# Retention queries projected ahead of the gates, attention's first keys and queries in memory of their own, pools waited for tile by tile, modulation sums spread

## The chip, the cores and the metric

The kernel runs on one core of a Trainium2 chip. A core has TensorE (PE, matrix products; its weight loads are listed as PEld), VectorE (DVE), ScalarE (ACT), GpSimd (POOL) and SyncE (SP, which here only issues DMAs), each with its own instruction stream that it works off in order, and 16 DMA engines that all queues share. The metric is the device time of one execution in microseconds (us).

## The reference

One layer of a diffusion backbone over 1024 latent tokens of width 1024, with 256 context tokens in front:

```
h      = rms_norm(x) * (1 + sc1) + sh1            # sc, sh, g: six vectors of silu(c) @ w_mod + b_mod
rq rk rv rg dq dk dv = split(h @ w_in)            # seven blocks of 512 columns, latents and context
y_ret  = silu(rg) * (retention forward + retention backward, each group-normed)   # 4 heads, chunks of 128
y_diff = subln((softmax(q1 k1) - lam * softmax(q2 k2)) @ v)                       # 4 heads, 1280 keys
x      = x + g1 * ([y_ret, y_diff] @ w_out)
x      = x + g2 * conv_ffn(rms_norm(x) * (1 + sc2) + sh2)                         # 1024 -> 2 x 2816 -> 1024
out    = rms_norm(x)
```

Retention walks through the chunks with a 128x128 state per head and direction: the forward and backward outputs of a chunk need its query, key, value, the state before it and the gate. The change touches only the part up to the end of the attention; the arithmetic stays the same.

## The kernel before, in words

Every product in float32 precision is made of three passes of 128x512 matmuls over a high and a low half of each operand (`passes`, L129 to L131). One tile of 128x512 outputs takes 8 x 3 of them.

**The first phase** (to about 100 us) computes two of the six modulation vectors (`pr`, `pm`), turns the latents (`px`), makes `hT`, the modulated input, and block 2 of `w_in` (retention values, tiles `pn`).

**The projections.** A block of `w_in` is streamed as four slices: a DMA into `raw` (2 buffers, pool `wr`), a cast on ACT to `whi` (L184) and a subtraction on DVE to `wlo` (L185), 5 buffers of that pair in pool `wp`. `natural` makes tiles with tokens on partitions and hands each to a finisher (`store_to`: one ACT copy, one DMA); `transposed` makes tiles with channels on partitions, which for queries and keys go through `rotated` (four ACT copies of 32 partitions, or two of 64, L419, and three DVE operations, L422 to L424; for the attention a cast on ACT, L410, and a subtraction on DVE, L411, too). All results go to DRAM. The blocks run in the order 5 (attention keys), 6 (attention values), 1 (retention keys), 3 (gates), 0 (retention queries), 4 (attention queries).

**Work beside the projections.** `beside(generator, rate)` gives a generator that much of a step for every group of three passes. `states_before` (backward states) runs beside block 3, `outputs` (the 32 retention steps) beside blocks 0 and 4, at 1.2 parts per group; a step has three parts. A step loads its query and key (`qk`) and its value and gate (`kvgf`), scores on PE (`pc`), decays on DVE (`sc`), multiplies with value and state (`po`), updates the state on PE and DVE (`puf`, `Sf`), and is gated on DVE and POOL (`o`, `ss`, `y`), turned (`pyt`) and stored (`yrd`). POOL makes `qq`, `ks`, the power for `ss`, and `y`.

**Modulation.** `modulation2(i)` for the other four vectors loads eight 512 KB pieces (`wm2`, 2 buffers), sums them on DVE into `macc` (1 buffer) and reduces over partitions on PE (`pg`) at once.

**The attention** has 32 units (4 heads of 8 query tiles): scores for the two maps (`pA`, one PSUM tile of 3 banks each), minimum on DVE (`mt`), exponential on ACT (`p`), their difference on DVE, turned on PE (`pt`), times the values (`pv`), normed and turned (`pty`). Their order is a table of phases. `load` fetches queries (`qhl`), keys (`ks`) and values (`va`) of a head on POOL's queue. The last `TAIL` = 2 tiles of block 4 are projected after the first unit's scores have been asked for.

**What sets the order.** A scheduler in the build places each engine's instructions (outside of stretches that `in_order` fixes) by priority and its own estimate of when operands are ready. Memory is given by pools stacked on a left and a right side; a pool opened where others were closed waits, as a whole, for those others.

## Time and profile before

| | us |
|---|---|
| median of 3 runs | 1436.45 |
| lowest, highest | 1434.34, 1439.01 |
| the profiled execution, its own time | 1439.18 |
| its span | 1437.4 |
| PE busy | 1378.5 (96%) |
| DVE, ACT, POOL busy | 1007.2, 732.1, 369.4 |

Busy time is the time an engine's records cover; matmuls are pipelined with modelled ends, so a covered PE can still run slowly. `PEclk` in a view by stretches is the clock granted to TensorE, 1.00 at full speed. A row of waits gives who waited, for what, the total in us, how often and the longest. In a timeline, the bracket behind a row has the engine's idle time before it and what ended it. By place in the program: first phase 0 to 103 us, projections to 350, projections with retention to 482, start of the attention to 517, attention to about 690, then output projection and feed-forward to the end.

### The profile page before, as it was taken

How to read it: one execution, taken by the hardware profiler on the slowest of the kernel's cores; microseconds unless marked ns; L12 is line 12 of the kernel's file. 1: busy time of each engine (PE TensorE's matmuls, PEld its weight loads, DVE VectorE, ACT ScalarE, POOL GpSimd, SP SyncE). 2: the span in 40 equal slices, each digit the busy share in tenths (PEclk: the TensorE clock that was granted, in tenths of full speed). 3: DMA queues.
4: the chain of work that ended last, by engine and by line, in shares of the span. 5: the costliest groups of instructions: out<-in, count | busy, mean ns of one | idle time of the engine just before them, and what ended most of it. 6: DMA issues, size and time to landing. Idle time of an engine off the chain costs nothing.

```text
span 1437.4 us, 19423 instructions
## 1 busy us (share of the span) xinstructions
PE 1378.5 (96%) x6924; PEld 1144.8 (80%) x6924; DVE 1007.2 (70%) x1499; ACT 732.1 (51%) x1398; POOL 369.4 (26%) x467
## 2 busy tenths in 40 slices
PE   6999999999899989999999999999999999999997
PEld 3678788787778779999888777888888888888886
DVE  3578724333577589889346997787777777998756
ACT  3535512322456588998314654555555445455433
POOL 1230000021788323431121143222232220024003
PEclk9999999999999999999999999999999999999999
DMA  8448765465455667570522223332223324963324
GB/s 334 154 161 272 262 200 188 135 198 183 136 169 180 185 153 167 139 151 1 198 74 88 73 82 110 110 110 91 87 95 110 110 96 157 397 215 116 132 96 147
DMA packets 106377, 217.77 MB, mean 152 GB/s; under 512 B 8804, under 2 KB 47204, under 8 KB 104360
## 3 DMA queue, kind: packets, MB, share of 16 engines
q1 hardware_dynamic: 98152, 191.62, 39.0%
q0 software_dynamic: 8128, 24.91, 7.6%
q8 instruction: 55, 0.90, 0.3%
q14 instruction: 42, 0.34, 0.1%
HBM read 159.08 MB, written 57.41 MB: 151 GB/s over the span
## 4 chain that ended last, share of the span: by engine, by line
PE 77%; DVE 8%; DMA 5%; issue 3%; POOL 3%; ACT 3%; SPq 0%; POOLq 0%; DVEq 0%; ACTq 0%
PE chain L129 5%; PE chain L130 5%; PE chain L131 5%; PE c L130 5%; PE c L131 5%; PE c L129 5%; PE pv L765 5%; PE pA L733 5%; PE pn L131 3%; PE pn L129 3%; PE pn L130 3%; PE third L130 2%; PE third L129 2%; PE third L131 2%; PE pt L753 2%
## 5 line engine op out<-in xcount | busy, mean ns | idle before, releaser
L129 PE MATMUL chain<-T,whi 128*128 128x512 f32 x264 | 103.7, 394 | 6.8 <-ACT ua L1135 4.3
L129 PE MATMUL pl<-hT,whi 128*128 128x512 f32 x256 | 107.2, 419 | 1.2 <-ACT whi L184 1.2
L130 PE MATMUL chain<-T,whi 128*128 128x512 f32 x264 | 103.5, 392 | 0.0
L131 PE MATMUL chain<-T,wlo 128*128 128x512 f32 x264 | 103.1, 391 | 0.0
L131 PE MATMUL pl<-hT,wlo 128*128 128x512 f32 x256 | 100.7, 394 | 0.3 <-DVE wlo L185 0.3
L130 PE MATMUL pl<-hT,whi 128*128 128x512 f32 x256 | 100.7, 393 | 0.0
L736 DVE TENSOR_REDUCE mt<-pA 128x1 f32<-128x1280 f32 x64 | 95.3, 1490 | 3.6 <-PE pA L733 2.0
L733 PE MATMUL pA<-ks,qhl 128*128 128x512 f32 (+1 forms) x384 | 92.0, 376 | 4.8 <-ACT p L740 4.8
L1048 POOL TENSOR_TENSOR cmb<-wrb 128x512 f32<-128x512 f32 x20 | 27.4, 1372 | 250.8 <-DMA wrb<-w_up 158.2
L131 PE MATMUL c<-whi,ghl 128*128 128x512 f32 x232 | 90.4, 390 | 0.0
L129 PE MATMUL c<-whi,ghl 128*128 128x512 f32 x232 | 90.3, 389 | 0.0
L130 PE MATMUL c<-wlo,ghl 128*128 128x512 f32 x232 | 90.3, 389 | 0.0
L740 ACT ACTIVATE p<-pA,mt 128x1280 f32<-128x1280 f32 x64 | 85.5, 1336 | 4.5 <-DVE mt L736 4.5
L899 ACT CAST whi<-cmb 128x512 fp32r<-128x512 f32 x62 | 38.6, 622 | 88.1 <-PE chain L130 65.2
L733 PEld LDWEIGHTS pA<-ks,qhl 128*128 128x128 f32 x384 | 69.2, 193 | 17.6 <-ACT p L740 5.9
L129 PE MATMUL pn<-whi,hT 128*128 128x512 f32 x192 | 80.0, 416 | 2.4 <-ACT hT L575 2.4
L765 PE MATMUL pv<-va,aT 128*128 128x128 f32 x640 | 77.0, 275 | 0.1
L131 PE MATMUL pn<-whi,hT 128*128 128x512 f32 x192 | 75.3, 396 | 1.6 <-DVE hT L577 0.9
L899 ACT CAST whi<-wra 128x512 fp32r<-128x512 f32 x55 | 33.7, 622 | 83.5 <-PE third L130 42.3
L130 PE MATMUL pn<-wlo,hT 128*128 128x512 f32 x192 | 75.8, 395 | 0.0
L765 PEld LDWEIGHTS pv<-va,aT 128*128 128x128 f32 x640 | 74.0, 192 | 0.7 <-DVE yT L794 0.3
L900 DVE TENSOR_TENSOR wlo<-cmb,whi 128x512 fp32r<-128x512 f32 x62 | 57.8, 934 | 23.7 <-ACT whi L899 23.7
(320 smaller groups left out, 3915.0 us busy)
## 6 DMA issues: line engine op xcount, KB each, us to landing
wm<-w_mod SPq DMA_DIRECT2D x32, 512.0 KB, 4.3
raw<-w_in SPq DMA_DIRECT2D x28, 512.0 KB, 4.3
wra<-w_up SPq DMA_DIRECT2D x24, 512.0 KB, 3.3
wrb<-w_up SPq DMA_DIRECT2D x23, 512.0 KB, 3.6
W<-w_down SPq DMA_DIRECT2D x44, 256.0 KB, 6.3
ad<-s SPq DMA_DIRECT2D x20, 512.0 KB, 3.6
wra<-ad SPq DMA_DIRECT2D x20, 512.0 KB, 3.3
wrb<-ad SPq DMA_DIRECT2D x18, 512.0 KB, 3.3
```

What stands on the lines that cost most here:

```text
L129: mm(ps, lh, rh, start=first, stop=False, skip_group_check=more)
L130: mm(ps, lh, rl, start=False, stop=False, skip_group_check=more)
L131: mm(ps, ll, rh, start=False, stop=last, skip_group_check=more)
L733: mm(self.pa[m][:, c0:c1], self.q[:, i, m, qs], self.k[:, m, c0:c1], start=(i == 0), stop=(i == 1))
L736: nc.vector.tensor_reduce(out=self.mt[:, m : m + 1], in_=self.pa[m][:, :LK], axis=AX.X, op=ALU.min)
L740: nc.scalar.activation(self.p[m], self.pa[m][:, :LK], AF.Exp, scale=-1.0, bias=self.mt[:, m : m + 1], accum_out=self.s[:, m : m + 1])
L753: nc.tensor.transpose(self.pt[g][:, i, :], self.p[0][:, (4 * g + i) * P : (4 * g + i + 1) * P], ident)
L765: mm(self.pv, self.aT[:, c, :], self.v[:, c, :], start=(c == 0), stop=(c == NKT - 1))
L899: nc.scalar.copy(hi, src)
L900: nc.vector.tensor_tensor(out=lo, in0=src, in1=r32(hi), op=ALU.subtract)
L1048: nc.gpsimd.tensor_tensor(out=s1, in0=b1, in1=b2, op=ALU.add)
```

## The change

- Block order becomes 5, 6 (context only), 1, 0, 3, 6 again (latents only), 4. So the retention queries are made before the gates, and the attention values of the latents are made beside the retention steps (rate 1.05 in place of 1.2). Block 6 is loaded and split twice.
- While blocks 5, 6, 1 and 0 run, pool `m2p` lends one more `raw` buffer and one more `whi`/`wlo` pair (3 and 6 in place of 2 and 5).
- `modulation2` only sums; `modulated2` does the reduction as a generator beside later projections. `macc` has 2 buffers, `wm2` 3.
- `raw_latents` loads all four tiles before it normalizes the first.
- Many pools get `reuse_waits="tile"`: a tile waits only for what lay at its own place.
- The attention's queries, keys and values get pools of their own (`aq0`, `aq1`, `ak0`, `ak1`, `av`) at the places where the weight buffers and retention states lay; three of the four state tiles move to a pool `sb`. The PSUM pools `pst1` and `psb1` swap sides, and the last four tiles of block 4 use only the two `psa1` banks.

```diff
+        raw_pools = [lambda: wr] * 2
+        slice_pools = [lambda: wp] * 5
         def split_slice(src):
-            raw = wr.tile([P, 2, 512], F32, name="raw")
+            n = next(n_slices)
+            raw = raw_pools[n % len(raw_pools)]().tile([P, 2, 512], F32, name="raw")
             nc.sync.dma_start(out=raw, in_=src)
-            whi = wp.tile([P, 2, 512], F32R, name="whi")
-            wlo = wp.tile([P, 2, 512], F32R, name="wlo")
+            pool = slice_pools[n % len(slice_pools)]()
+            whi = pool.tile([P, 2, 512], F32R, name="whi")
+            wlo = pool.tile([P, 2, 512], F32R, name="wlo")
...
-            acc = m2p.tile([P, D], F32, name="macc")
+            maccs[i] = acc = m2p.tile([P, D], F32, name="macc", bufs=2)
...
+        def modulated2(i):
+            acc = maccs.pop(i)
             if i in (0, 3):
...
+                    yield
...
             def raw_latents():
+                xs = []
                 for t in range(4):
-                    xt = xp.tile([P, D], F32, name="xt", bufs=5)
-                    nc.sync.dma_start(out=xt, in_=x[t * P : (t + 1) * P, :])
-                    yield
+                    xs.append(xp.tile([P, D], F32, name="xt", bufs=5))
+                    nc.sync.dma_start(out=xs[t], in_=x[t * P : (t + 1) * P, :])
+                yield
+                for t, xt in enumerate(xs):
                     normalize(xt, 2 + t)
...
-        m2p = m2c.enter_context(tc.tile_pool(name="m2p", bufs=1))
+        m2p = m2c.enter_context(tc.tile_pool(name="m2p", bufs=1, reuse_waits="tile"))
+        raw_pools.append(lambda: m2p)
+        slice_pools.append(lambda: m2p)
         rtab = load_rope(1)
         wg = stream_block(5)
+        modulation2(0)
...
-        modulation2(1)
         transposed(wg, dk_d, rtab, 32, 1.0, LC, by_head[3:])
         wg = stream_block(6)
+        beside(modulated2(0), 0.1)
         natural(wg, ctx_lhs, range(NTC), store_to(dv_row))
-        modulation2(0)
-        natural(wg, lat_lhs, range(NT), store_to(dv_row, c0=NTC))
...
         wg = stream_block(1)
+        rtab = load_rope(0)
+        natural(wg, ctx_lhs, range(NTC), store_to(kvg_row(0), scale=RET_SCALE))
+        beside(iter(()), 0.0)
+        modulation2(1)
+        transposed(wg, [q[:, 1] for q in rqk_d], rtab, 64, RET_SCALE, 0, by_head[:5], True)
+        beside(modulated2(1), 0.4)
         modulation2(2)
-        natural(wg, ctx_lhs, range(NTC), store_to(kvg_row(0), scale=RET_SCALE))
+        transposed(wg, [q[:, 1] for q in rqk_d], rtab, 64, RET_SCALE, 0, by_head[5:], True)
+        wg = stream_block(0)
+        beside(modulated2(2), 0.25)
         modulation2(3)
+        transposed(wg, [q[:, 0] for q in rqk_d], rtab, 64, 1.0, 0, by_head[:6])
+        beside(modulated2(3), 0.2)
+        transposed(wg, [q[:, 0] for q in rqk_d], rtab, 64, 1.0, 0, by_head[6:])
...
-        transposed(wg, [q[:, 1] for q in rqk_d], rtab, 64, RET_SCALE, 0, by_head, True)
+        sb = rtx.enter_context(tc.tile_pool(name="sb", bufs=H - 1, side="right", reuse_waits="tile"))
         wg = stream_block(3)
         beside(states_before(), 36 / 62)
         natural(wg, lat_lhs, range(NT), store_to(kvg_row(2), func=AF.Silu, c0=NTC))
-        wg = stream_block(0)
-        beside(outputs(), 1.2, -12.0)
-        transposed(wg, [q[:, 0] for q in rqk_d], rtab, 64, 1.0, 0, by_head)
+        wg = stream_block(6)
+        beside(outputs(), 1.05, -12.0)
+        natural(wg, lat_lhs, range(NT), store_to(dv_row, c0=NTC))
         rtab = load_rope(1)
         wg = stream_block(4)
-        transposed(wg, dq_d, rtab, 32, -DIFF_SCALE, 0, by_head[:-TAIL])
+        transposed(wg, dq_d, rtab, 32, -DIFF_SCALE, 0, by_head[: -TAIL - 2])
+        mm_tiles[0] = itertools.cycle([ps_a])
+        transposed(wg, dq_d, rtab, 32, -DIFF_SCALE, 0, by_head[-TAIL - 2 : -TAIL])
...
-        al = aload.enter_context(tc.tile_pool(name="al", bufs=2, side="right"))
+        aq0, ak0, av, aq1, al, ak1 = (loads(*args) for args in (("aq0",), ("ak0",), ("av", 2), ("aq1",), ("al", 2), ("ak1",)))
...
-                cur["k"] = al.tile([P, 2, LK], F32R, name="ks")
+                cur["k"] = (ak0, ak1)[h % 2].tile([P, 2, LK], F32R, name="ks")
-                cur["q"] = al.tile([P, 2, 2, 4 * P], F32R, name="qhl")
+                cur["q"] = (aq0, aq1)[qt // 4].tile([P, 2, 2, 4 * P], F32R, name="qhl")
```

ACT at the start of the program, before (`sq` squares an input tile, `xraw` takes a turned tile out of PSUM, `rw` takes the first modulation sum, `whi` is the first weight slice):

```order
L520 ACTIVATE sq,sm<-xt 128x1024 x2
L567 COPY xraw<-px 128x4x128
L520 ACTIVATE sq,sm<-xt 128x1024
L567 COPY xraw<-px 128x4x128 x2
L507 COPY rw<-pr 128x512
L520 ACTIVATE sq,sm<-xt 128x1024
L184 CAST whi<-raw 128x1024
```

and now:

```order
L533 ACTIVATE sq,sm<-xt 128x1024 x2
L582 COPY xraw<-px 128x4x128
L533 ACTIVATE sq,sm<-xt 128x1024
L582 COPY xraw<-px 128x4x128
L533 ACTIVATE sq,sm<-xt 128x1024
L582 COPY xraw<-px 128x4x128 x2
L520 COPY rw<-pr 128x512
L190 CAST whi<-raw 128x1024
```

The fourth square has moved from behind `rw` to ahead of it.

POOL near the end of the retention, before: the last two steps' work, then all loads of the first attention head (`qhl` queries, `ks` keys, `va` values).

```order
L115 TENSOR_TENSOR ss<-ss,mhalf 128x2
L298 TENSOR_TENSOR y<-o 128x128
L299 TENSOR_TENSOR y<-y,kvgf 128x128
L811 DMA qhl<-dq_86 64x4x512 x2
L815 DMA ks<-dk_90 64x1280 x4
L818 DMA va<-dvd 128x10x128
L811 DMA qhl<-dq_86 64x4x512 x2
```

and now, with the first of these loads nine steps (by `qq`) before the retention's end:

```order
L844 DMA qhl<-dq_86 64x4x512
L115 TENSOR_TENSOR ss<-ss,mhalf 128x2
L261 TENSOR_TENSOR qq<-qk,qd 128x256
L236 TENSOR_SCALAR ks_4103<-kvgf,kd 128x128
L261 TENSOR_TENSOR qq<-qk,qd 128x256
L844 DMA qhl<-dq_86 64x4x512
L115 TENSOR_TENSOR ss<-ss,mhalf 128x2
L304 TENSOR_TENSOR y<-o 128x128
L236 TENSOR_SCALAR ks_4150<-kvgf,kd 128x128
L305 TENSOR_TENSOR y<-y,kvgf 128x128
L261 TENSOR_TENSOR qq<-qk,qd 128x256
L848 DMA ks<-dk_90 64x1280
```

Six loads (two of `qhl`, four of `ks`) now stand between retention steps on POOL; `va` and the second half of the queries stay behind the last step.

On PE the first unit's two sets of scores stood 10 passes before the end of block 4 and right behind it; now they stand 48 and 33 passes before its end.

SP where block 5 is about to start, before (`raw` is the fourth slice of block 5, `wm` the pieces of a modulation sum, `kvg` stores of retention values):

```order
L403 DMA kvg_82<-st 128x512
L458 DMA macc<-rows 1x1024
L461 DMA wm_1183<-w_mod 128x1024
L403 DMA kvg_82<-st 128x512
L461 DMA wm_1186<-w_mod 128x1024
L646 DMA lp<-rows 128x256
L647 DMA lg<-rows 128x8
L461 DMA wm_1189<-w_mod 128x1024
L650 DMA dec<-consts 128x1024
L461 DMA wm_1192<-w_mod 128x1024
L403 DMA kvg_83<-st 128x512
L181 DMA raw<-w_in 128x1024
```

and now:

```order
L409 DMA kvg_82<-st 128x512
L186 DMA raw<-w_in 128x1024
L466 DMA macc<-rows 1x1024
L409 DMA kvg_82<-st 128x512
L469 DMA wm_953<-w_mod 128x1024
```

The fourth slice has moved ahead of the first modulation piece.

48 lines of the change are left out of this document (27 added, 21 removed).

## The prediction

> **What bounds the kernel now.** I read the page first: PE is covered almost everywhere, so a gain can come only from places where PE waits or runs slowly.
>
> ```profile
> span 1437.4 us, 19423 instructions
> PE   6999999999899989999999999999999999999997
> PEclk9999999999999999999999999999999999999999
> ```
>
> The change ends with the attention, so the second half (slices 20 to 40) stays out. Next the waits of PE, longest first. All the rows below lie ahead of 517 us; those of the feed-forward, of the first load and some small ones are left out.
>
> ```profile
> PE po L278 <- DVE Sf L237: 6.0, 7, 1.5
> PE pA L733 <- ACT p L740: 4.8, 5, 2.4
> PE px L564 <- DVE xt L522: 4.3, 2, 3.4
> PE pn L129 <- ACT whi L184: 2.4, 1, 2.4
> ...
> PE pc L271 <- DMA qk<-rqk: 2.1, 1, 2.1
> PE pyt L303 <- POOL y L299: 1.8, 3, 1.3
> PE pg L467 <- DVE macc L462: 1.6, 1, 1.6
> PE pl L129 <- ACT whi L184: 1.2, 1, 1.2
> ...
> PE puf L290 <- DVE sc L273: 0.9, 1, 0.9
> ...
> PE pk L435 <- DVE xa L424: 0.9, 1, 0.9
> ...
> PE po L278 <- DVE sc L273: 0.5, 1, 0.5
> ```
>
> These eleven rows sum to 26.5 us. No single one is large: the kernel loses its time at some twenty places. But a wait costs more than its length. The view by stretches, cut where the granted clock (third column from the right) changes, shows half speed right behind the longest waits:
>
> ```profile
> 23.61:30.44 6.83, 6.83 (x28) 4.67 (x26) 3.23 (x8) 1.73 (x3) 1.28 (x1) 0.50 0.75 269
> 173.80:177.21 3.41, 3.41 (x10) 2.63 (x9) 1.61 (x2) 1.50 (x2) 0.00 (x0) 0.50 0.96 377
> 361.53:364.94 3.41, 3.41 (x16) 3.10 (x15) 0.78 (x3) 0.35 (x1) 0.67 (x2) 0.50 0.54 157
> 504.89:511.72 6.83, 5.28 (x15) 4.21 (x16) 6.83 (x9) 3.25 (x6) 0.00 (x0) 0.50 0.25 88
> ...
> 517.00:683.00 166.00, 165.96 (x1234) 154.89 (x1233) 148.24 (x201) 151.08 (x353) 50.16 (x95) 1.00 0.56 123
> ```
>
> PE's busy time at half clock is half lost: 3.4, 1.7, 1.7 and (5.28 busy) 2.6 us, together 9.4, which the page's clock row is too coarse to show. The last row is the steady attention, where PE works 165.96 of 166 us: nothing is to be had there.
>
> **The change part by part.**
>
> *First phase.* ACT takes the first modulation sum (`rw`) ahead of the fourth input tile, and with it PE stands still:
>
> ```profile
> 19.72 0.59 ACT L507 COPY rw<-pr 128x512 f32<-128x512 f32 x1 [2.16 <-PE pr L503]
> 20.20 1.06 ACT L520 ACTIVATE sq<-xt 128x1024 bf16<-128x1024 f32 x1
> ```
>
> ```profile
> 23.10 1.47 PE L564 MATMUL px<-ident,xt 128*128 128x128 f32 x8 [3.45 <-DVE xt L522]
> ...
> 27.86 0.80 PE L129 MATMUL pn<-whi,hT 128*128 128x512 f32 x1
> ```
>
> Now the square is ahead, so the 3.45 us of standing go. But the eight turns (1.47) now stand ahead of the sum on PE, and the sum's chain starts that much later: the first `pn` comes about 2.0 us sooner. If PE no longer stands still, the half clock of 23.61 to 30.44 goes too, and of its 3.4 us I count 2.5. I take 4.5; bounds 0 (the loads, which cover 0.75 of the engines there, are late instead) and 6.9 (both in full).
>
> *Weight slices.* The chain of waits shows two slices that come late:
>
> ```profile
> 106.65 5.50 DMA raw<-w_in
> 112.17 1.05 ACT whi L184
> ...
> 165.36 1.15 DVE wlo L185
> 166.52 4.74 DMA raw<-w_in
> 171.28 1.05 ACT whi L184
> ```
>
> At 165.36 a slice is split as soon as the block before lets go of its place; only that frees the `raw` buffer, so the next DMA starts at 166.52 and PE waits for it. With six pairs and three buffers all four slices of the next block are loaded beforehand, and only splits (1.05 and 1.15) remain, in the last chain's 24 passes. Both waits go: 1.2 + 2.4, and the 1.7 of clock behind the second: 5.3. Bounds 0 and 5.3.
>
> The Trainium skill ("TensorE: Matmul & The Clock Gate", section "What's actually happening") lets the clock fall only after an idle window of about 3.4 us. By that the gaps of 2.4 and 2.1 us would cost no clock, and the sum would be 3.4 us smaller; the rows at 173.80 and 361.53 show half clock behind just these gaps, so I go by them.
>
> *Modulation sums.* `pg` waits 1.6 for the last sum, `pk` 0.9 for a rotated tile whose turn is the last thing in its block. Sums now end a block before they are reduced, and the last turn of block 1 falls beside block 0. 2.5; bounds 0 and 2.5. The 32 additions stay on DVE.
>
> *Retention queries.* `qk` waits 2.1 because it reads what was stored a moment before; the queries are now stored a whole block earlier. With the clock behind it (361.53): 3.8. Bounds 0 and 3.8.
>
> *Retention steps.* `po`, `pyt` and `puf` wait 6.0 + 1.8 + 0.9 + 0.5 = 9.2. DVE works its stream in order, and three rotations of 0.7 to 0.8 us stand in front of the small state operations, seven times in this stretch (357 to 437):
>
> ```profile
> L424 DVE TENSOR_TENSOR xa<-xa,xb 128x512 f32<-128x512 f32 x7 | 5.6, 797 | 0.1
> L422 DVE SCALAR_TENSOR_TENSOR xa<-pl,rtab 128x512 f32<-128x512 f32 x7 | 4.8, 686 | 3.0 <-ACT xb L419 2.9
> L423 DVE TENSOR_TENSOR xb<-xb,rtab 128x512 f32<-128x512 f32 x7 | 4.8, 681 | 0.0
> ```
>
> Beside block 6 there are none; about half of the steps now run there, the others beside block 4, whose tiles are rotated and split. Half of 9.2 is 4.6; the thinner spread (1.05 for 1.2) helps a little more, but crowding beside block 4 takes that back. 4.5; bounds 0 and 9.2.
>
> *Start of the attention.* The store of a rotated query tile lands late, since all loads of the first head are under way at once; ACT stands behind it and the first exponential comes after that:
>
> ```profile
> 488.60 11.54 DMA dq<-xhl
> ...
> 500.88 1.43 ACT p L740 x2
> ```
>
> ```profile
> 498.02 0.40 PE L129 MATMUL pl<-hT,whi 128*128 128x512 f32 x1
> 498.25 0.40 PE L130 MATMUL pl<-hT,whi 128*128 128x512 f32 x1
> ```
>
> 4.8 are lost as waits (the `pA` row) and 2.6 as clock (the row at 504.89): 7.4. Now the first unit's scores stand 48 and 33 passes ahead of the end; passes start 0.23 apart, as the two rows show, so 33 of them cover 7.6 us of its softmax. What the second and third unit wait for each other remains, for which I leave 2.5. Gain 4.9; bounds 2 and 7.4. The last tiles of block 4 have two PSUM banks in place of five; a tile takes 24 x 0.23 = 5.5 us to make, in which the other bank is emptied, so nothing for that. The swapped sides and the waits tile by tile are what lets scores and loads stand where they do, and are in these terms.
>
> Sum of gains: 4.5 + 5.3 + 2.5 + 3.8 + 4.5 + 4.9 = 25.5 us.
>
> *What it adds.* Block 6 is loaded and split a second time: four times 1.05 on ACT and 1.15 on DVE, beside PE passes; DVE and ACT are far from full there, so nothing. If that cover were gone it would be 8.8. The blocks behind the retention queries have five pairs again: two changes of block (to 6 and to 4), each between 0 and the 4.1 of the one at 170; I take half, 4.1. POOL gets six loads between retention steps:
>
> ```profile
> 485.04 1.61 POOL L811 DMA_DIRECT2D qhl<-dq  x2 [4.78 <-DMA yrd<-yr]
> 486.53 2.21 POOL L815 DMA_DIRECT2D ks<-dk  x4
> ...
> 437.00:482.00 45.00, 41.92 (x248) 34.88 (x248) 31.59 (x89) 28.34 (x94) 32.58 (x57) 1.00 0.44 147
> ```
>
> 3.8 us of issuing on an engine that is busy 32.58 of 45 us there, with `qq`, `ks`, `ss` and `y` behind it, which PE needs a step later. The first must also wait until a stored query tile has landed. Bounds 0 and the rival below; I take 3.8. Net: 25.5 - 4.1 - 3.8 = 17.6 us.
>
> **The rivals.**
>
> *Half of it.* PE's waits move rather than go: only what rests on memory and order is saved (slices 5.3, `qk` 3.8, `pg` and `pk` 2.5, together 11.6), while first phase, steps and start stay, and 4.1 at the changes of block come in: 7.5 us. For it: DVE is 31.59 of 45 busy beside block 4 (437 to 482), where half of the steps will run, and small waits are spread over many engines. Against it: the standing in the first phase and at the start has one cause each that the order takes away. Median 1429.
>
> *Slower: POOL's queue is blocked.* A load at the head of POOL's queue waits for a store, and all retention work on POOL behind it. Price: a store took 11.54 us at worst (row at 488.60); two loads read such stores, 23.1, and 3.8 of issuing make 26.9. POOL's spare share, 12.4 of 45, works off 9 of it in the nine steps left (a step takes some 3.8: 32 of them from about 360 to 482), and one step's length is cover; so 14 to 23 reach PE, and two standstills cost up to 3.4 of clock each. At the upper end that is 23.1 + 6.8 = 29.9, against 25.5 of gain: 4.4 slower, and 8.5 with the 4.1 at the changes of block. It decides from a loss of about 21 us. Against it: other stores land far sooner, and the big loads that made that one late are now spread. Median 1442.
>
> The Trainium skill ("DMA: Bandwidth & Descriptors", section "SWDGE vs HWDGE vs iDMA") says that GpSimd writes its descriptors into SBUF, from which DVE can lock it out. By that these issues, now beside a busy DVE, would be slower than the 0.6 to 0.8 us above; no row here shows a load issued there, and the chance of this rival has a little of that in it.
>
> *No change.* The gaps close up elsewhere, because each stage is paced by DVE or POOL anyway. The 11.6 that rest on memory and order then meet the 3.8 of issuing and the upper bound at both changes of block, 8.2: nothing is left. For it: POOL is busy 72% of the retention beside block 4. Against it: of the six changes of block before, with five pairs, only two cost over 1 us. Median 1436.
>
> **How the numbers follow.** The profiled execution took 1439.18 us with a span of 1437.4; the median of the runs is 1436.45, 2.7 below that execution. So the span should be near 1437.4 - 17.6 = 1419.8, and the median 1436.45 - 17.6 = 1418.85, told as 1419. Chances: the forecast 0.64, half of it 0.20, slower 0.09, no change 0.07. The least that can be told from no change is 0.3%, 4.3 us. The forecast and half of it are faster: 0.84; slower 0.09; same 0.07. The forecast's own range is 1408 to 1426 (some, not all, of the terms at one bound); with half of it and its spread the range reaches 1434.
>
> **What would show it.** Right: no `px` wait of 3 us and no half clock near 25 us; no `whi` waits near 110 and 170; no `pg` and `qk` rows among PE's waits; DVE's `Sf` row at 2 to 3 us; at most two half-clock stretches ahead of the attention; last projection to first `pv` about 5 us shorter. Wrong: POOL idle in front of `qhl` or `ks` during the retention with `pyt` or `po` behind `y`, `qq` or `ks`; new `whi` waits at the second block 6 or at block 4; a standstill of PE in the first phase that only moved.

## The result, and the profile after

Five runs of each on one chip: before 1436.45 us (median; 1432.08 to 1439.01), changed 1426.36 us (1425.03 to 1430.19). The ratio is 0.9936, with a 95% interval from 0.9912 to 0.9961: faster by 10.1 us, where 17.6 had been predicted. The median lies 0.4 us outside the forecast's own range (1408 to 1426) and inside the whole one (to 1434). The profiled execution of the changed kernel is the median run itself (1426.36, span 1424.6); that of before was 2.7 us above its median, so between the two profiles 12.8 us are to be explained.

The page of the changed kernel:

```profile
span 1424.6 us, 19441 instructions
PE   6899999999999899999999999999999999999997
PEclk8999999999999999999999999999999999999999
```

PE is covered as before; the clock row is one step lower in its first slice. The waits of PE up to 520 us (who waited, for what; total, times, longest), without the first load of the program:

```profile
PE pn L129 <- ACT hT L590: 3.7, 4, 1.8
PE pA L766 <- ACT p L773: 3.6, 3, 1.9
PE pk L441 <- DVE xa L430: 2.3, 2, 1.9
...
PE puf L296 <- DVE sc L279: 2.1, 4, 0.7
...
PE pt L786 <- ACT aT L792: 1.4, 1, 1.4
PE pyt L309 <- POOL y L305: 1.3, 1, 1.3
...
PE pt L541 <- DVE xc L535: 1.1, 1, 1.1
...
PE po L284 <- DVE Sf L243: 0.7, 3, 0.3
```

The rows for `whi`, `pg` and `qk` are gone; `po` behind the states fell from 6.0 to 0.7. `pk` grew from 0.9 to 2.3 and `aT` from 0.6 to 1.4; new are `xc` and small waits in the steps. The first row grew too. It was already there in the kernel before, as long as the longer of the two `whi` rows:

```profile
PE pn L129 <- ACT hT L575: 2.4, 3, 1.0
```

The view by stretches, cut at the changes of the granted clock (a stretch, its length, the busy time of PE, of its weight loads, of DVE, ACT and POOL with their instructions, then the clock, the DMA share and GB/s):

```profile
23.99:30.82 6.83, 6.24 (x18) 3.25 (x19) 2.08 (x3) 1.16 (x2) 1.27 (x1) 0.50 0.61 211
...
58.12:61.54 3.42, 3.20 (x9) 2.36 (x10) 2.54 (x4) 1.90 (x5) 2.52 (x3) 0.50 0.00 0
504.50:670.50 166.00, 165.97 (x1234) 154.91 (x1233) 148.60 (x201) 150.69 (x353) 52.81 (x99) 1.00 0.61 136
```

No half clock is left between 61.54 us and the attention (before: at 173.80, 361.53 and 504.89), but the one of the first phase stayed and another came at 58. (A window of half clock from 17.16 to 20.58 lies where the kernel before had not yet reached full clock, which it did at 20.20.) The steady attention (last row) is as before.

Where the 12.8 us lie, stretch by stretch. "Over the work" is a stretch's length less what its PE instructions take from one start to the next elsewhere (the median for each shape, over all the profiles of this study); since the trace lacks a few records, it is good to some tenths.

| stretch of the program | length before | length now | over the work before | now |
|---|---|---|---|---|
| first phase, to the first tile of block 5 | 106.74 | 107.72 | 24.6 | 25.8 |
| block 5 and context keys | 58.42 | 55.35 | 1.5 | 0.2 |
| context tiles of blocks 6 and 1 | 27.93 | 23.74 | 5.1 | 0.6 |
| retention keys (block 1) | 50.48 | 51.09 | 3.4 | 3.2 |
| before: values alone; now: queries alone | 45.63 | 48.65 | -0.8 | 2.0 |
| gates with backward states | 54.12 | 54.65 | 4.4 | 5.3 |
| from there to the first retention score | 16.76 | 11.10 | 2.9 | 0.0 |
| steps, to the last turn `pyt` | 120.56 | 125.51 | 25.9 | 19.9 |
| from there to the first `pv` | 36.37 | 26.54 | 8.5 | 6.0 |
| sum, to the first `pv` | 517.01 | 504.35 | 75.4 | 62.9 |

From the first `pv` on nothing changed: 920.4 us before, 920.3 now.

### The profile page after: what moved, and what is told of

It is laid out like the page before. It is cut to its first block, busy times and chain, and to the rows that moved or that the text cites. A ratio compares the mean times of both kernels' runs of the same rounds, so it can differ in the third digit from the quotient of the medians.

```text
span 1424.6 us, 19441 instructions
## 1 busy us (share of the span) xinstructions
PE 1372.8 (96%) x6924; PEld 1141.5 (80%) x6924; DVE 1009.1 (71%) x1503; ACT 735.3 (52%) x1402; POOL 358.9 (25%) x467
## 4 chain that ended last, share of the span: by engine, by line
PE 44%; issue 3%; DMA 2%; DVE 2%; ACT 1%; POOL 0%; POOLq 0%; DVEq 0%; ACTq 0%
PE chain L129 5%; PE chain L130 5%; PE chain L131 5%; PE c L131 4%; PE c L130 4%; PE c L129 4%; PE third L131 2%; PE third L130 2%; PE third L129 2%; PE po L131 2%; PE po L130 2%; PE po L129 2%; DMA W<-w_down 1%; PE second L130 1%; PE second L131 1%
## 5 line engine op out<-in xcount | busy, mean ns | idle before, releaser
L130 PE MATMUL chain<-T,whi 128*128 128x512 f32 x264 | 103.5, 392 | 0.0
L129 PE MATMUL pn<-whi,hT 128*128 128x512 f32 x192 | 84.5, 441 | 3.7 <-ACT hT L590 3.7
L425 ACT ACTIVATE xb<-pl 32x512 f32<-32x512 f32 (+1 forms) x96 | 56.7, 590 | 52.9 <-PE pl L131 28.6
L131 PE MATMUL pn<-whi,hT 128*128 128x512 f32 x192 | 76.4, 401 | 0.8 <-POOL hT L548 0.4
```

Source lines behind the costliest of these rows:

```text
L129: mm(ps, lh, rh, start=first, stop=False, skip_group_check=more)
L130: mm(ps, lh, rl, start=False, stop=False, skip_group_check=more)
L131: mm(ps, ll, rh, start=False, stop=last, skip_group_check=more)
L425: nc.scalar.activation(xb[q * blk : (q + 1) * blk, :], pt[o : o + blk, :], AF.Copy, scale=scale)
```

## The experiments

Each was timed against the kernel before on the same chip. The chips differ (the kernel before took 1433.05 to 1436.45 us on them), so two kernels are best compared by their ratios. Theory: in the first phase PE's standing only moved; the block order won more than predicted because the two added costs were smaller; the start is held by the rotation of the last query tiles. Rivals stand with each run. All edits are to the changed kernel.

| kernel | median, us | ratio to before | 95% interval |
|---|---|---|---|
| changed | 1426.36 | 0.9936 | 0.9912 to 0.9961 |
| e1, old loading of the first tiles | 1423.70 | 0.9909 | 0.9889 to 0.9930 |
| e2, five slices | 1427.95 | 0.9947 | 0.9927 to 0.9967 |
| e3, old block order | 1433.15 | 0.9993 | 0.9976 to 1.0010 |
| e4, old start | 1430.33 | 0.9958 | 0.9946 to 0.9970 |
| e5, turns behind the first product | 1421.14 | 0.9914 | 0.9890 to 0.9937 |
| e6, second sum earlier | 1432.05 | 0.9979 | 0.9960 to 0.9997 |
| e7, value tiles last | 1425.63 | 0.9938 | 0.9920 to 0.9957 |
| e8, attention loads on SP | 1423.34 | 0.9925 | 0.9907 to 0.9943 |
| e9 = e5 + e8 | 1417.55 | 0.9885 | 0.9868 to 0.9901 |
| e10 = e9 + e7, uneven spread | 1421.48 | 0.9916 | 0.9900 to 0.9932 |
| e11, few sums | 1425.08 | 0.9932 | 0.9913 to 0.9952 |
| e12 = e9, start filled | 1418.40 | 0.9882 | 0.9854 to 0.9910 |

An interval is some 3 us to either side, so single edits of 1 to 3 us can't be told apart by these times: against the changed kernel only e3 (slower), e9 and e12 (faster) have an interval wholly clear of its own. For the others the stretches of the profiles are read, one profiled execution of each.

### e1: the first tiles loaded as before

```diff
-                xs = []
                 for t in range(4):
-                    xs.append(xp.tile([P, D], F32, name="xt", bufs=5))
-                    nc.sync.dma_start(out=xs[t], in_=x[t * P : (t + 1) * P, :])
-                yield
-                for t, xt in enumerate(xs):
+                    xt = xp.tile([P, D], F32, name="xt", bufs=5)
+                    nc.sync.dma_start(out=xt, in_=x[t * P : (t + 1) * P, :])
+                    yield
                     normalize(xt, 2 + t)
```

> The changed kernel with the loading of the first four latent tiles written as before (each tile loaded and normalized one after the other, so the first modulation sum is copied ahead of the fourth tile's square); all else as changed. Theory (read off the two profiles): this edit brings the first pass (pn) forward by 3.3 us (27.9 to 24.6) but the half clock stays and a new one at 58 us joins it, so that block 5 begins 1.0 us later than before; undone, block 5 begins at 106.7 +- 0.5 in place of 107.7, no half clock at 58, and the time is about 1 us under the changed kernel's 1426.4. Rival (as predicted): the edit is worth 4.5 us and another part of the change took it away in this stretch; then the time rises by 3 to 5 us and block 5 begins near 111.

Block 5 begins at 105.46 us, sooner than expected; seven other kernels with the new loading (e2, e3, e4, e6, e7, e8, e11) begin it at 106.7 to 107.6. The kernel before, with the same old loading, begins it at 106.74, but its first full clock comes at 20.20 us, that of e1 at 15.47. Set beside profiles of the new loading with a full clock about as early (106.7 to 107.7) and about as late (107.1 to 107.6), the old loading is sooner in both cases, by 1.2 to 2.3 and 0.4 to 0.8 us. So the edit gained nothing and cost 0.4 to 2.3 us. One part of the expectation fell: half clock stands at 56.43 to 59.84 here too. PE in the changed kernel, with the idle time ahead of a row in brackets:

```profile
15.53 1.06 PE L579 MATMUL px<-ident,xt 128*128 128x128 f32 x8 [1.25 <-DVE xt L535]
17.61 1.94 PE L579 MATMUL px<-ident,xt 128*128 128x128 f32 x8 [1.01 <-DVE xt L535]
19.48 1.58 PE L516 MATMUL pr<-wt,wide 128*32 128x512 f32 x8
21.77 1.05 PE L523 MATMUL pm<-fold,rw 128*128 128x2 f32 x8 [0.71 <-ACT rw L520]
24.58 0.80 PE L129 MATMUL pn<-whi,hT 128*128 128x512 f32 x1 [1.76 <-ACT hT L590]
```

The 3.45 us in front of the fourth tile are gone, but the product `pr` now stands behind all the turns. It no longer fills the time between the turns of the third and the fourth tile (1.25 and 1.01 of standing), and nothing is left to put into the sum's chain (`rw`, `pm`, the first `hT`: 0.71 and 1.76). Together that is 4.7 us, against 0.86 and 3.45 before. The first pass does come sooner (24.58 for 27.86), but the half clock stays (row 23.99 above) and now lies on passes (and one `pr`) from 24.58 on, where before turns, `pm` and `pr` filled its stretch up to 27.86. At 57 a second thing came in. DVE before, then DVE now:

```profile
55.47 0.75 DVE L522 TENSOR_SCALAR xc<-xc,sm 128x1024 f32<-128x1024 f32 x1 [0.66 <-POOL sm L115]
56.28 0.16 DVE L514 TENSOR_TENSOR mcol<-pm,bsc 128x4 f32<-128x4 f32 x1
```

```profile
56.15 0.16 DVE L527 TENSOR_TENSOR mcol<-pm,bsc 128x4 f32<-128x4 f32 x1 [1.25 <-PE pm L523]
...
56.43 0.75 DVE L535 TENSOR_SCALAR xc<-xc,sm 128x1024 f32<-128x1024 f32 x1
```

The scheduler put the context tile's scaling behind an instruction that waits for PE, and PE then waits 1.1 us for the tile (the `xc` row). With the old loading the order is the old one again: a side effect of that edit.

### e5: the fourth tile's turns behind the first product

```diff
-                for t, xt in enumerate(xs):
-                    normalize(xt, 2 + t)
+                for t in range(3):
+                    normalize(xs[t], 2 + t)
+                for t, xt in enumerate(xs):
+                    if t == 1:
+                        normalize(xs[3], 5)
...
-            beside(raw_latents(), 1.5, 1.0)
+            beside(raw_latents(), 0.875, 1.0)
```

> The changed kernel with the first four latent tiles loaded at once as changed, but each tile normalized ahead of the turns of the one before and the turns spread thinner (0.875 for 1.5), so that the first modulation product (pr) stands on PE ahead of the fourth tile's turns again while the four squares stay ahead of the sum's copy (rw) on ACT. Theory (PE's standing in the first phase only moved: 4.3 us ahead of and behind the fourth tile's turns in the kernel with the old loading, 4.7 us around pr, pm and the first pn in the changed one): with the turns between pm and the first pn the standing falls by 1.5 to 2.5 us, the first pn comes at 22 to 23 us in place of 23.3 to 24.6, block 5 begins at 105 +- 0.7 in place of 106.7 to 107.7; time 1424 to 1425. Rival (the loads set the pace here, as the lower bound of the prediction says): the start of block 5 does not move by more than 0.5 us and PE waits for wt (DMA) more than at its first product.

Block 5 begins at 101.68 us, and in the three later kernels with this edit (e9, e10, e12) at 103.5, 103.1 and 104.0: on the mean 4 us sooner than in the eight profiles of the changed kernel's first phase, more than expected. The profiled execution of e5 was the fastest of its four (1415.81 us, the median is 1421.14), so the other three are the better measure. PE in e5:

```profile
16.80 1.07 PE L516 MATMUL pr<-wt,wide 128*32 128x512 f32 x8
18.57 1.05 PE L523 MATMUL pm<-fold,rw 128*128 128x2 f32 x8 [0.70 <-ACT rw L520]
19.48 1.07 PE L582 MATMUL px<-ident,xt 128*128 128x128 f32 x8
20.48 1.06 PE L516 MATMUL pr<-wt,wide 128*32 128x512 f32 x8
22.92 0.50 PE L129 MATMUL pn<-whi,hT 128*128 128x512 f32 x1 [1.37 <-ACT hT L593]
```

Turns and the next product now lie inside the sum's chain, and in none of the four kernels is there half clock near 25 us. The `xc` wait of 1.1 us is gone as well: the context tile's scaling stands in its old place again, so about 1 of the 4 us is not the turns'. So the loads did not set the pace here; the order did. This is what the prediction had counted on the change to do.

### e2: five slices

```diff
-        raw_pools.append(lambda: m2p)
-        slice_pools.append(lambda: m2p)
...
-        raw_pools.pop()
-        slice_pools.pop()
```

> The changed kernel without the third raw buffer and the sixth pair of slices. Theory: the waits for whi and the half clock behind the second of them come back: block 5 and the two context pieces behind it take 5 to 6 us longer than the 55.4 and 23.7 us of the changed kernel; time 1426.4 + 5 to 6 = 1431 to 1433. Rival: in the new order of blocks the slices would have been early with five pairs too (the order saved the waits); then the time stays within 1 us and no whi wait over 1 us is in the profile.

Between block 5 and the first retention score the stretches come to 13.7 us over their work, against 11.2. The waits up to 242 us, and the clock behind the longer of them:

```profile
PE pn L129 <- ACT whi L190: 2.9, 2, 2.0
PE pk L441 <- DVE xa L430: 0.5, 1, 0.5
```

```profile
179.40:182.81 3.41, 1.45 (x7) 0.98 (x6) 1.18 (x1) 2.25 (x3) 0.38 (x1) 1.00 0.50 197
182.81:186.22 3.41, 3.41 (x10) 2.63 (x9) 3.17 (x4) 0.23 (x1) 0.00 (x0) 0.50 0.66 187
```

The wait and its clock return at the context tiles (6.0 over the work against 0.6), as the theory says. Block 5 has 0.3 us where it had 1.2 before, so that part did not need the sixth pair; what took it away was not run by itself. Of the 5.4, some 2.9 come back behind: `pk` waits less, and so do the backward states. The buffers are worth about 2.5 us, not 5 to 6.

### e3: the old block order

```diff
-        wg = stream_block(6)
-        beside(outputs(), 1.05, -12.0)
-        natural(wg, lat_lhs, range(NT), store_to(dv_row, c0=NTC))
+        wg = stream_block(0)
+        beside(outputs(), 1.2, -12.0)
+        transposed(wg, [q[:, 0] for q in rqk_d], rtab, 64, 1.0, 0, by_head)
```

(The latents' values stand behind the context's again, and the sums beside blocks 6 and 1.)

> The changed kernel with the blocks in their old order (values of the latents straight behind those of the context, retention queries beside the outputs, spread 1.2); buffers, first phase and start as changed. Theory: the query wait comes back with its clock (3.8 as predicted, 4.7 as the two profiles differ), and the steps' waits beside the queries (6.5 in the profile before, 0.9 now beside the values of the latents): 8 to 10 us in all, less what the second loading of a block costs now (0 as the profile shows): 1434 to 1436. Rival (as predicted): the two changes of block with five pairs cost 4.1 now, so undoing gives them back, 1426.4 + 8.3 - 4.1 = 1430.6.

6.8 us slower by the medians, 8 by the ratios. The waits of PE from 338 to 476 us:

```profile
PE po L284 <- DVE Sf L243: 6.0, 7, 1.5
...
PE pc L277 <- DMA qk<-rqk: 0.9, 1, 0.9
```

The `Sf` row is the old one to the tenth: rotations in front of the state operations, gone in the changed kernel and back with the old order. The query wait of the first step is 0.9, not 2.1, and brought no half clock. From the context tiles to the last turn the stretches are 36.7 us over their work against 30.9 now: the order is worth 5.8, less than the 8 to 10 expected, and the start takes 1.1 of it back.

### e4 and e8: the old start, and the loads on SP

```diff
-        aq0, ak0, av, aq1, al, ak1 = (loads(*args) for args in ...)
-        pss = {m: loads(f"pss{m}", space=PSUM) for m in (1, 0)}
+        al = aload.enter_context(tc.tile_pool(name="al", bufs=2, side="right"))
+        pss = {1: aload.enter_context(tc.tile_pool(name="pss1", bufs=1, space=PSUM, side="right"))}
...
-        mm_tiles[0] = itertools.cycle([ps_a])
```

> The changed kernel with the attention's pools as before (keys, queries and values in one pool of two buffers, pools waited for as a whole, five PSUM banks for the last tiles). Theory: the start costs 8.5 us over its work again in place of 6.0, so 2.4 us are lost, and the six loads that POOL now issues between retention steps beside block 4 (4.0 us of issuing) leave that stretch, which as the profile shows gives back 0 to 1 us: 1427.8 to 1428.8. Rival (as predicted): 4.9 lost at the start and 3.8 won back in the steps, 1427.5, told apart by the two stretches: waits of PE beside block 4 fall from 6.0 to about 2, start 4.9 longer.

The expectation had the price wrong: the start is 14.6 us over its work, not 8.5. Here PE's first `pA` waits for the pool as a whole:

```profile
PE pA L762 <- DVE xhl L417: 6.9, 1, 6.9
```

So in the new block order the attention's own pools and the waits tile by tile, undone here together, save some 8.5 us, though against the kernel before the start gained only 2.4. And the steps beside block 4 fall from 13.6 to 10.9 us over their work once the six loads no longer stand between them. e8 asks for that alone:

```diff
+            eng = nc.gpsimd if i else nc.sync
...
-                    nc.gpsimd.dma_start(out=cur["q"][...], in_=...)
+                    eng.dma_start(out=cur["q"][...] if i else r32(cur["q"][...]), in_=...)
```

> The changed kernel with the first six loads of queries and keys issued by SP in place of POOL. Theory: POOL's 4.0 us of issuing beside block 4 is what makes the steps 2.7 us slower there than with the old start (13.6 us over the work against 10.9); without it they fall to 11 to 12, unless SP's queue stands behind the loads: 1424 to 1425. Rival: the two PSUM banks for the last tiles or the DMA traffic of the loads make the difference; then 13 to 14 stays, 1426.

10.9 us again. With POOL issuing, the five profiles beside the changed one that leave this part alone (e1, e2, e5, e6, e11) show 11.7 to 13.5; without it (e4, e8, e9, e12) 10.9 to 11.2: POOL's issuing costs 0.5 to 2.7 us, 1.8 on the mean. In the changed kernel POOL's timeline shows how:

```profile
443.39 0.62 POOL L848 DMA_DIRECT2D ks<-dk  x1
444.07 0.71 POOL L115 TENSOR_TENSOR ss<-ss,mhalf 128x2 f32<-128x2 f32 x1
444.75 0.44 POOL L304 TENSOR_TENSOR y<-o 128x128 f32<-128x128 f32 x1
445.15 0.58 POOL L848 DMA_DIRECT2D ks<-dk  x1
...
461.49 0.69 POOL L115 TENSOR_TENSOR ss<-ss,mhalf 128x2 f32<-128x2 f32 x1 [1.89 <-DMA qk<-rqk]
```

No idle time in front of a load, so the queue was never blocked by a store; the loads take their 0.6 to 0.9 us each. But they have a second effect, in the last row: a step's own load (`qk`), issued by SP at 453.33, landed 8.1 us later, and POOL stood 1.89 us for it. Such a load took 7.6 to 11.3 us at worst in e1, e2, e5 and e6, and at most 5.3 in e4, e8, e9 and e12. How much of the 1.8 us is POOL's own time and how much these late loads, no run tells.

### e7: value tiles at the end

```diff
+        rtab = load_rope(1)
+        wg = stream_block(4)
+        beside(outputs(), 1.05, -12.0)
+        transposed(wg, dq_d, rtab, 32, -DIFF_SCALE, 0, by_head)
         wg = stream_block(6)
-        beside(outputs(), 1.05, -12.0)
-        natural(wg, lat_lhs, range(NT), store_to(dv_row, c0=NTC))
+        natural(wg, lat_lhs, range(NT - TAIL - 2), store_to(dv_row, c0=NTC))
...
-        transposed(wg, dq_d, rtab, 32, -DIFF_SCALE, 0, by_head[-TAIL:])
+        natural(wg, lat_lhs, range(NT - TAIL, NT), store_to(dv_row, c0=NTC))
+        values(0, NKT - TAIL, NKT)
```

> The changed kernel with the attention queries made ahead of the second loading of the values block: all eight query tiles stand beside the first half of the retention steps, and the two tiles that cover the first unit's softmax are value tiles (one ACT copy each, no rotation); the last two rows of values are loaded by a DMA of their own behind them. Theory: of the 6.0 us that the start of the attention still costs, about half is DVE and ACT time of rotating and splitting the two query tiles (on DVE four operations of 0.68, 2.7 us a tile, between the minima of the first units); the start falls to 3 to 4 us, the steps stay within 1.5 us: 1423.5 to 1425.5. Rival: the start is the first units' own chain (scores, minimum, exponential, difference, turns) with one PSUM tile per map, and stays at 5.5 to 6 us; then 1426 or more, with the steps slower by up to 2 us for the two more tiles to rotate beside them.

The start falls to 3.0 us over its work, as the theory says. DVE at the start of the changed kernel, then of e7:

```profile
492.32 1.49 DVE L769 TENSOR_REDUCE mt<-pA 128x1 f32<-128x1280 f32 x1
493.73 0.68 DVE L430 TENSOR_TENSOR xa<-xa,xb 128x512 f32<-128x512 f32 x1
494.33 0.68 DVE L428 SCALAR_TENSOR_TENSOR xa<-pl,rtab 128x512 f32<-128x512 f32 x1
494.93 0.68 DVE L429 TENSOR_TENSOR xb<-xb,rtab 128x512 f32<-128x512 f32 x1
495.53 1.49 DVE L769 TENSOR_REDUCE mt<-pA 128x1 f32<-128x1280 f32 x1
```

```profile
492.28 2.89 DVE L769 TENSOR_REDUCE mt<-pA 128x1 f32<-128x1280 f32 x2 [6.99 <-PE pA L766]
496.74 1.49 DVE L769 TENSOR_REDUCE mt<-pA 128x1 f32<-128x1280 f32 x1 [1.58 <-PE pA L766]
```

In the changed kernel the second minimum stands behind three operations of rotations; in e7 it follows the first at once. But the steps pay it back: 22.2 us over the work in both stretches, against 19.9. The eight tiles must be rotated somewhere, and DVE is where the steps are late too.

### e6 and e11: the sums

```diff
         natural(wg, ctx_lhs, range(NTC), store_to(dv_row))
+        modulation2(1)
...
-        modulation2(1)
```

> The changed kernel with the second of the four modulation sums (the one that was put ahead of the retention keys) begun behind the context values, so that DVE has done its eight additions before the first retention key is rotated. Theory: the new wait of pk for a rotated tile (1.9 us in the changed kernel, 1.3, 0.5 and 0 in others) is caused by additions that stand ahead of the rotation on DVE and wait for their pieces; it goes, the waits ahead of the gates fall to under 0.7 us, and the key block shortens by 1 to 2 us: 1424.5 to 1425.5. Rival: the additions meet the weight slices there instead (a whi wait of over 1 us in the two context pieces) and nothing is gained.

This failed twice over. The rival came true (1.4 for `whi`, 1.1 for `wlo` and half clock at 179: the sum's pieces are loaded ahead of the slices), and the `pk` wait stayed, because the edit moved the wrong sum. The additions ahead of the first key rotations are those of the third sum, in the changed kernel too: its eight stand at 188 to 201 us there (189 to 205 in e6), those of the second already at 143 to 159 (126 to 147 in e6), since the scheduler had put them forward. DVE of e6:

```profile
199.51 1.28 DVE L470 SCALAR_TENSOR_TENSOR macc<-wm,csil,macc 128x1024 f32<-128x1024 f32 x1 [3.30 <-DMA wm<-w_mod]
200.71 0.68 DVE L428 SCALAR_TENSOR_TENSOR xa<-pl,rtab 128x512 f32<-128x512 f32 x1
```

An addition waits 3.30 us for its piece with the rotation that `pk` needs behind it. So e11 took the additions away:

```diff
-            for k in range(KD):
+            for k in range(1):
                 wt = m2p.tile([P, D], F32, name="wm2", bufs=3)
```

> The changed kernel with 28 of the 32 pieces of the four modulation sums left out (neither loaded nor added; each sum has its first piece alone), so that nearly no addition stands ahead of a rotation. Theory: the retention key and query blocks lose 6.0 us over their work (3.6 and 2.4) of which the pk wait (1.9) and part of the rest are these additions and their late pieces; without them 3 to 4 us stay: 1423.5 to 1425. Rival: pk waits for its own rotation chain; 1.5 to 2 us of pk wait stay and the two blocks keep their length.

No wait of PE is listed from 186 to 284 us, and keys and queries come to 2.8 us over their work against 5.1: 2.3 us less than in the changed kernel's profile. But the cost varies: with all sums, the first `pk` waits 1.9 us in the changed kernel and in e6, 0.5 to 1.5 in e1, e2, e5, e7, e8, e10 and e12, and not at all in e4 and e9; in e4 keys and queries take the same 97.4 us as in e11. It hangs on when the pieces land: the last addition that waits for one ahead of that rotation starts 4.4 us before `pk` in the changed kernel, in e1 and in e6. So the additions cost 0 to 2.3 us. The edit takes their loads away too, and the medians (1425.08 against 1426.36) can't be told apart.

### e9 and e10: what adds up

> The two edits of e5 (fourth tile's turns behind the first modulation product) and e8 (first six attention loads issued by SP) together on the changed kernel. Theory: they touch different places (first phase; steps beside block 4) and add up: 1426.4 - 4 to 5 - 3 = 1418 to 1420, block 5 at 101.5 to 105, steps beside block 4 at 10.8 +- 0.7 us over their work. Rival: one of the two was luck of the clock's windows or of the chip; then 1421 to 1423.

1417.55 us, ratio 0.9885 (0.9868 to 0.9901): the gains of e5 and e8 stand side by side (block 5 begins 4.2 us sooner than in the changed kernel, the steps stay at the value without POOL's issuing), and this beats both kernels.

```diff
-        beside(outputs(), 1.05, -12.0)
+        beside(outputs(), 0.85, -12.0)
...
         wg = stream_block(6)
+        side["rate"] = 1.4
```

> e9 with the order of e7 (attention queries ahead of the second values block, value tiles last), and with the retention steps spread 0.85 beside the queries and 1.4 beside the values in place of 1.05 throughout. Theory: the start stays at 3.0 us over its work as in e7; what e7 lost in the steps (22.2 us over the work in both stretches against 19.7) came from rotations and steps meeting on DVE in the first half, and the uneven spread brings it to 18 to 20: 1 to 4 us below e9. Rival: the steps are paced by their own chain wherever they stand; denser steps beside the values wait more, and the sum of both stretches stays at 21 or more: no gain over e9.

The rival: the start is 3.2, but the steps are 26.3 us over their work, against 17.4 in e9, and 22.2 in e7, which has this order with the even spread. PE's waits in them (334 to 478 us):

```profile
PE puf L296 <- DVE sc L279: 4.5, 5, 1.4
PE po L284 <- DVE Sf L243: 4.4, 7, 1.2
PE pc L277 <- ACT o L287: 2.1, 1, 2.1
```

The rows are the steps' own chain (decay, state, gating), and the even spread is better.

### e12: the start filled with useless products

```diff
+            def fill(self, m, n):
+                for _ in range(n):
+                    mm(self.pa[m][:, LK:1536], self.q[:, 0, m, 0:P], self.k[:, m, 0:256], start=True, stop=True)
...
+                    if op == "S0" and u in (1, 2):
+                        units[u].fill(0, 12 if u == 1 else 8)
```

> e9 with useless products put where PE stands at the start of the attention: 12 matmuls of 128x256 (keys times queries of unit 1, into the 256 columns of its PSUM tile that nothing reads) behind the second unit's scores, 8 behind the third's. Theory (the clock is set anew every 3.41 us, to half for the next such window if PE stood idle for about 1.8 us or more of the one before): the 1.87 us gap there shrinks to under 0.6 us, no window near the start has 1.6 us of idle time and no half clock follows the start, whatever the phase of the windows (e9: two half windows, 2.9 us lost; 8 of the 12 profiles with that start had one): the start falls from 7.3 us over its work to about 4.5 (the products themselves counted as gaps filled), the time from 1417.5 to 1415.5 to 1417. Rival (clock falls behind a gap of some length, or for another reason): half clock at the start in spite of it, or the products delay the units as much as they save: 1417.5 or more.

The stretches of the clock's own windows at the start, e9 and then e12:

```profile
483.86:487.28 3.42, 1.55 (x8) 1.17 (x7) 3.42 (x5) 2.93 (x5) 0.00 (x0) 1.00 0.00 0
487.28:490.69 3.41, 3.41 (x13) 2.71 (x12) 3.41 (x4) 1.93 (x3) 0.00 (x0) 0.50 0.19 73
...
494.10:497.52 3.42, 3.42 (x13) 3.03 (x13) 1.90 (x2) 2.29 (x5) 2.56 (x6) 0.50 0.26 79
```

```profile
484.89:488.30 3.41, 2.96 (x21) 2.55 (x20) 3.41 (x5) 2.82 (x5) 0.00 (x0) 1.00 0.00 0
488.30:491.72 3.42, 2.31 (x15) 1.85 (x14) 3.42 (x5) 1.93 (x3) 0.00 (x0) 1.00 0.22 88
...
495.13:498.54 3.41, 3.41 (x29) 3.24 (x27) 2.67 (x5) 3.00 (x5) 2.56 (x6) 1.00 0.31 99
```

The half clock is gone at the start, as the theory says. The gain in time is not there: 1418.40 against 1417.55 (ratios 0.9882 and 0.9885), nothing that can be told apart. From the first `pA` to the first `pv` e12 takes 26.7 us and e9 28.0, but the changed kernel, whose windows happened to fall well, took 26.7 too, and e1 and e5 took 26.7 in spite of one window at half clock each. e6 and e8 with one took 27.7, e11 with two 28.1. So half speed there costs 0 to 1.4 us, not the 3.4 that it shows (half of PE's 3.41 and 3.42 us in e9's two rows at 0.50; the expectation's 2.9 was taken from the next column, the weight loads). That the rest falls into time in which PE would wait anyway is argued, not shown.

## Why the prediction was wrong in size and right in direction

| term | predicted gain, us | between the two profiles |
|---|---|---|
| first phase | 4.5 | -1.1 |
| weight slices (block 5, context tiles) | 5.3 | 5.8 |
| modulation sums (keys) | 2.5 | 0.3 |
| block order: queries 3.8, steps 4.5, less 4.1 and 3.8 | 0.4 | 5.1 |
| start of the attention | 4.9 | 2.4 |
| sum | 17.6 | 12.5 |

The right column is the difference of the table by stretches, before rounding (so single rows can be 0.1 off); the block order is its rows from "values alone" to the steps (32.3 to 27.2), taken together because the queries carry their own 2 us from the steps into a place of their own. The lengths give 12.7 for 12.5. What is left to the 10.1 of the medians is that the profiled execution of before lay 2.7 us above its median.

**First phase: the step that failed.** "If PE no longer stands still, the half clock of 23.61 to 30.44 goes too, and of its 3.4 us I count 2.5." I took the standing away where I saw it and did not follow it on. Three things went against that step: the standing moved (4.7 us for 4.3, of it 2.5 behind the turns), the half clock stayed and lay on more passes, and the scheduler's order of the context scaling flipped. The row that would have warned, the passes' 2.4 us behind `hT`, was left out of the prediction's list of waits; it grew to 3.7. The sign named for this, "a standstill of PE in the first phase that only moved", is what the profile shows. In the four kernels with e5's edit block 5 begins 2.7 to 5.1 us earlier than in the kernel before, so most of the 4.5 was there to be had, by an order in which the turns stay inside the sum's chain; the change's order pulled them out.

**Slices: right for the whole, for another reason in part.** The waits and the clock behind the second went. But e2 gives the sixth pair only 2.5 us: the wait of block 5 went without it, and what it saves at the context tiles is partly lost at `pk` and the states.

**Sums: mis-sized.** `pg` went (1.6), but `pk` grew (0.9 to 2.3). I had looked at where the last turn stands, not at what stands ahead of its rotation on DVE: additions that wait for pieces just loaded. e11 prices the additions there, with their loads, at 0 to 2.3 us.

**Block order: the mechanism right, the costs too high.** The rows beside the values block fell as predicted: `po` behind `Sf` is back at 6.0 in e3. DVE's `Sf` row, forecast at 2 to 3 us, is 0.7. But PE's waits beside block 4 came to 6.0 us, where the prediction had left 4.7 for all the steps. And the two added costs were set too high: no `whi` wait stands at the second block 6 or at block 4 (0 for 4.1), and POOL's issuing cost 0.5 to 2.7 for 3.8. The Trainium skill ("DMA: Bandwidth & Descriptors", section "SWDGE vs HWDGE vs iDMA") has GpSimd write descriptors into SBUF, from which DVE in one of its modes locks it out. The rows at 443.39 and 445.15, with DVE at work (in which mode, no view tells), show no such delay: 0.62 and 0.58 us, against 2.21 for four before. The rival of a blocked queue did not come: no load waited at the head of POOL's queue. Late loads did come in part, as a step's `qk` behind the six.

**Start: half of it.** The scores do stand early, and the first unit's softmax is covered. I left 2.5 us for what the second and third unit wait for each other; it was 5.0 of standing (rows of 3.6 and 1.4). Missing from my step was that the tiles used as cover bring their own rotation to DVE, between the minima. e7 shows that this is half of the 6.0.

Of the rivals, "half of it" named the time best (7.5 gained, 10.1 measured), and its reason holds in part: waits moved, in the first phase, at `pk`, in the steps and at the start. Not its details: the changes of block cost nothing, and steps and start did gain. That the sum came as near as it did is partly luck: 4.7 us too little at the block order stand against 5.6 too much in the first phase.

## What to carry to other kernels

When a wait is taken away by changing an order, follow the chain to the next thing that PE needs and ask what now lies inside it: work that was pulled ahead no longer covers it. Work used as cover must be cheap on the engines that the covered chain runs on. And an addition that waits for a DMA holds everything behind it on its engine (3.30 us in e6); look up in the trace which one stands there before moving any, since the scheduler may already have moved the one that the program text suggests.

## What the runs showed of the hardware

**The clock is granted in windows of their own.** The changes of the clock stand 3.41 us apart or a multiple of it, in every profile, and the first step to full speed lies at 13.75 us in the changed kernel, at 15.47 in e1 and at 20.20 in the kernel before: the windows do not start with the program. Counted over all fourteen profiles, behind the first phase and ahead of the program's end: of 34 windows at full clock in which PE stood idle for 1.86 us or more, 32 were followed by half clock; of 10 with 1.60 to 1.86 us, 3; of 76 with 0.9 to 1.6 us, none. So the same gap can cost a window of half speed or nothing. The gap of 1.87 us at the start of the attention lies whole in one window in e1, e3, e5 and e9, and half clock follows; in the changed kernel and in e2 a border cuts it into 1.59 and 0.29, and 1.75 and 0.12 us, and none follows. In the first phase, where PE has many small products, less standing was enough (1.46 us in the window in front of 58.12, in which `pm` also ran for 0.95). The Trainium skill ("TensorE: Matmul & The Clock Gate", section "What's actually happening") says that the window is 3413 ns long and free-running, which these rows bear out, and that the clock falls after an idle window; here a window that was idle for little more than half was enough.

This is also why a term of half clock should be taken as a chance and not as a fixed price: in eight profiles of the same first phase the standing in front of the first pass was followed by two windows of it (six profiles) or by one (e6 and e8), and block 5 began between 106.7 and 107.7 us.
